# Layer A's attention: block scores inside each tile's near score products, block values inside the near value batch, outputs in the two halves of one PSUM bank

## The chip, the core and the metric

The kernel runs on one core of one Trainium2 chip. The metric is device time in microseconds (us) of one execution; less is better. The engines: PE multiplies matrices (PEld are its weight loads), DVE is the vector engine, ACT the scalar engine with the exponential, POOL the general one, SP issues most of the DMA transfers. Every engine works through its own row of instructions in a fixed order and waits on semaphores for the others. SBUF is the on-chip memory of 128 partitions; PSUM, in eight banks of 128 x 512 float32, takes what PE computes.

## What is computed

A decoder trunk of two layers over x of 1 x 1024 x 1024 (float32). Layer A has a sparse attention with three branches, layer B a dilated attention across shared keys; after each stands a SwiGLU. The change touches layer A's attention alone:

```
def nsa_attention(h, ...):                    # 16 heads of 64, in 4 groups that share keys
    ...
    k_cmp = compress(kvh(kc), pe_k, w1_k, w2_k)         # 63 blocks of 32 tokens, stride 16
    v_cmp = compress(kvh(vc), pe_v, w1_v, w2_v)
    s = einsum('bsgrd,bngd->bgrsn', q, k_cmp) * scale   # block scores
    p, denom, _ = masked_softmax(s + bias_c, dist_c >= 0)
    p_cmp = p / maximum(denom, 1e-30)
    o_cmp = einsum('bgrsn,bngd->bsgrd', p_cmp, v_cmp)   # block values
    imp = einsum('bgrsn,nj->bgsj', p_cmp, overlap)      # what a query makes of each 64-token block
    score = where(forced, imp + FORCE_BONUS, where(blk_j <= cur, imp, -1.0))
    _, sel_idx = top_k(score, 8)
    ...                                                 # o_sel: attention to the 8 chosen blocks ("far")
    o_win, _ = banded_attention(q, kwn, vwn, 255, 1, rel_bias)    # the last 256 tokens ("near")
    o = g[..., 0:1] * o_cmp + g[..., 1:2] * o_sel + g[..., 2:3] * o_win
    return o @ w_out
```

## The kernel before

Layer A's attention runs over 32 units: 4 groups g of heads by 8 tiles t of 128 queries. A unit has four heads, taken in two pairs hp. Queries and keys are kept as a high and a low part in the reduced format fp32r. The high and low part of a query stand above each other on 128 partitions (Q); a key part is loaded twice, into both halves of the partitions, so that two products (key part high, key part low) with the same Q give the full score.

`cmp_job` (L709) makes a unit's block scores: four products of plain float32, Q against the 63 block keys kc (L718, 128x64), two heads to a score bank; DVE adds the bias C and takes the row minimum (L726), ACT the exponential (L730), POOL scales by gate and denominator (L740, L741). From tile 4 on a chain of small DVE instructions ranks the blocks and writes the mask mk (L745 to L756), PE turns it (L758) and ACT copies it into the queries' extra rows QM (L759). `dense_job` (L769) makes two heads' scores of one branch: near (br = 2, at most three key blocks; L795 and L796 against the tiles KW) or far (br = 1; the tiles K with KF or QM); DVE adds the bias T or TW (L798), ACT takes the exponential (L804), POOL scales (L808). A job's second half, `back()`, comes later: `values` (L345) turns the weights P block by block on PE (`turned`, L327, into a pt bank), DVE and ACT by turns copy them to the tiles pT (L330), and PE multiplies by the value block, one product for each of the two head pairs, onto 64 partitions each (L361). The block values have a product of their own over all 128 partitions (L765), which opens the output bank. Outputs go through two banks "o"; DVE copies them to oT (L818).

Score banks are three, pt banks three. Near keys come by `load_kw`: once for tiles 0 to 3 of a group (512 columns), once for tiles 4 to 7 (768 columns). The order is that of `jobs()`: near pair 0, the next unit's block scores, near pair 1, far pairs 0 and 1, with back halves two jobs later; a scheduler then interleaves the engines' rows from this order and from its own costs. Layer B's attention further on uses the same `values` and `turned`, and writes its outputs to the two halves of one bank (copy at L1641).

Of the kernel before, what the change touches and what calls it, by code (L numbers as in the profile page):

```python
# [24 lines left out]
G = 4  # L25
# [90 lines left out]
def trunk(ctx, tc, I, out):  # L116
# [206 lines left out]
    def turned(p, heads, copy):  # L323

        ps = bank("pt")
        for i, h in enumerate(heads):
            prev = nc.tensor.transpose(ps[:, i * 128:(i + 1) * 128], h, ident)  # L327
        w = len(heads) * 128
        t = p.tile([128, 512], F32, name="pT", bufs=6)
        copy(t[:, :w], ps[:, :w])  # L330
        return t, prev
# [13 lines left out]
    def values(p, po, Ps, vs, first, last, behind=None):  # L345
# [5 lines left out]
        for lo, hi in zip([0] + ends, ends):  # L351
# [6 lines left out]
            for b in reversed(range(lo, hi)):  # L358
                with after(prev), after(behind if lo == 0 and b == hi - 1 else None):
                    for e in range(2):  # L360
                        mm = nc.tensor.matmul(po[64 * e:64 * e + 64, :256], vs[b], ts[b - lo][:, e * 256:(e + 1) * 256],  # L361
                                              start=first and lo == 0 and b == hi - 1, stop=last and hi == nb and b == lo,
                                              skip_group_check=True)
                prev = mm
# [29 lines left out]
    kc = ares.tile([128, G, DH], F32, name="kc")  # L394
# [5 lines left out]
    with ExitStack() as c:  # L400
# [98 lines left out]
        def compress(i, kc2, weights):  # L499
# [25 lines left out]
            if i == 0:  # L525
# [8 lines left out]
                nc.vector.tensor_copy(kc, ps2.rearrange("p (g n) -> p g n", n=DH))  # L534
# [96 lines left out]
    with ExitStack() as c:  # L631
# [8 lines left out]
        rKw = [Ring(f"KW{i}", [128, (512, 768)[i]], F32R, [((kA0, kA1)[i], 2)]) for i in range(2)]  # L640
# [3 lines left out]
        rW = Ring("TW", [128, 384], F32, [(kA1, 4), (kB, 1)])  # L644
# [57 lines left out]
        pcs = [wk.tile([128, 4, 64], F32, name=f"pc{i}") for i in range(2)]  # L702
        units = [(g, t) for g in range(G) for t in range(NT)]
        po_, weights = {}, [None, None]
# [6 lines left out]
        def cmp_job(g, t):  # L711
            C = grp["C", g]
            nv = min(8 * t + 7, 63)
            psv = []
            for hp in range(2):
                ps = bank("s")[:].rearrange("p (e n) -> p e n", e=2)
                for e in range(2):
                    nc.tensor.matmul(ps[:, e, :DH], f32(query(g, t, 2 * hp + e)), kc[:, g, :], start=True, stop=True)  # L718
                    psv.append(ps[:, e, :])
            pc = pcs[(g * NT + t) % 2]  # L720
            pv = pc[:, :, :nv]
            nc.gpsimd.memset(pc[:, :, nv:64], 0.0)
            mx = wk.tile([128, 4], F32, name="cm", bufs=3)
            dn = wk.tile([128, 4], F32, name="cd", bufs=3)
            for hh in range(4):
                nc.vector.tensor_tensor_reduce(out=pc[:, hh, :nv], in0=psv[hh][:, :nv],  # L726
                                               in1=C[:, hh, 56 - 8 * t:56 - 8 * t + nv], scale=1.0, scalar=3e38,
                                               op0=OP.add, op1=OP.min, accum_out=mx[:, hh:hh + 1])
# [13 lines left out]
            if t >= 4:  # L742
# [13 lines left out]
                nc.vector.tensor_scalar(mk, s2_, -2e38, BIG, op0=OP.is_gt, op1=OP.mult)  # L756
                mt = bank("pt")
                nc.tensor.transpose(mt[:16, :128], mk, ident)  # L758
# [3 lines left out]
            def back():  # L762
                pT, _ = turned(wk, [pc[:, 2 * c:2 * c + 2, :] for c in range(2)], nc.vector.tensor_copy)
                po = po_[g, t] = bank("o")
# [3 lines left out]
        def dense_job(g, t, br, hp):  # L768
# [42 lines left out]
            def back():  # L811
                if hp == 0:
                    return
# [1009 lines left out]
```

## Time and profile before

| | us |
|---|---|
| median of 3 runs (2864.04 to 2868.19) | 2866.13 |
| the profiled execution | 2866.31 |
| its span, first to last instruction | 2864.5 |
| layer A's attention in it, 280.34 to 697.67 | 417.33 |
| PE busy in this stretch | 408.87 |
| DVE, ACT, POOL busy in it | 327.54, 290.34, 221.64 |

In the profile's rows a group is named by line, engine and operation, out<-in by tile names, count, busy time and mean duration; behind the bar stands the idle time ahead of it and what ended that. In the order of time, a row is start, duration, engine, line, tiles, count, and in brackets a wait with its releaser. A wait row reads: who waited for whom, us in total, times, longest. A product of plain float32 has two records (so 128 block-score products are 256 records); a transpose has one.

### The profile page before, as it was taken

How to read it: one execution, taken by the hardware profiler on the slowest of the kernel's cores; microseconds unless marked ns; L12 is line 12 of the kernel's file. 1: busy time of each engine (PE TensorE's matmuls, PEld its weight loads, DVE VectorE, ACT ScalarE, POOL GpSimd, SP SyncE). 2: the span in 40 equal slices, each digit the busy share in tenths (PEclk: the TensorE clock that was granted, in tenths of full speed). 3: DMA queues.
4: the chain of work that ended last, by engine and by line, in shares of the span. 5: the costliest groups of instructions: out<-in, count | busy, mean ns of one | idle time of the engine just before them, and what ended most of it. 6: DMA issues, size and time to landing. Idle time of an engine off the chain costs nothing.

```text
span 2864.5 us, 43332 instructions
## 1 busy us (share of the span) xinstructions
PE 2782.1 (97%) x14686; PEld 2256.2 (79%) x14686; DVE 2248.1 (78%) x4563; ACT 1441.3 (50%) x3173; POOL 1463.9 (51%) x1502
## 2 busy tenths in 40 slices
PE   9999999999999999999999999999989999999997
PEld 8988777776778888888777788787767788888886
DVE  5443877877878989998885877588888788888987
ACT  5432767775563433343364444577756434343434
POOL 3135555553666555655557777210026656655552
PEclk9999999999999999999999999999999999999999
DMA  8669143112222232222223555776450221112112
GB/s 234 210 206 325 44 107 81 42 42 107 85 63 67 67 81 69 61 68 69 63 89 112 157 157 162 243 236 183 127 177 19 74 60 55 56 52 63 52 45 78
DMA packets 276030, 307.02 MB, mean 107 GB/s; under 512 B 39676, under 2 KB 210733, under 8 KB 275808
## 3 DMA queue, kind: packets, MB, share of 16 engines
q1 hardware_dynamic: 255344, 241.26, 28.5%
q0 software_dynamic: 20464, 62.99, 6.9%
q8 instruction: 116, 1.90, 0.3%
q14 instruction: 106, 0.87, 0.1%
HBM read 237.93 MB, written 81.95 MB: 112 GB/s over the span
## 4 chain that ended last, share of the span: by engine, by line
PE 79%; DVE 9%; DMA 3%; POOL 3%; issue 3%; ACT 2%; SPq 1%; POOLq 0%; DVEq 0%; ACTq 0%
PE ux L1071 16%; PE uy L1071 13%; PE dx L923 7%; PE o L361 6%; PE pt L327 6%; PE dr L923 5%; PE mm L203 3%; PE mm L204 3%; PE mm L205 3%; DVE pl L884 2%; PE s L795 2%; PE dr L1071 2%; PE s L796 2%; PE dx L1071 1%; PE s L1671 1%
## 5 line engine op out<-in xcount | busy, mean ns | idle before, releaser
L884 DVE TENSOR_TENSOR pl<-oT,ph 128x512 fp32r<-128x512 f32 x337 | 354.6, 1069 | 68.8 <-PE dr L923 17.4
L883 ACT ACTIVATE ph<-oT 128x512 fp32r<-128x512 f32 x347 | 211.8, 627 | 198.4 <-PE ux L1071 50.1
L808 POOL TENSOR_SCALAR P<-P,sm,gates 128x384 f32<-128x384 f32 (+7 forms) x256 | 182.1, 723 | 118.0 <-DVE sm L806 98.2
L884 DVE TENSOR_TENSOR pl<-oTb,ph 128x512 fp32r<-128x512 f32 x233 | 213.7, 939 | 28.3 <-PE dr L923 17.2
L883 ACT ACTIVATE ph<-oTb 128x512 fp32r<-128x512 f32 x239 | 145.5, 627 | 167.9 <-PE ux L1071 52.1
L327 PE MATMUL pt<-ident,P 128*128 128x128 f32 x1536 | 223.1, 278 | 2.2 <-DVE pT L330 1.5
L928 DVE TENSOR_TENSOR xr<-xr,dr 128x512 f32<-128x512 f32 x320 | 203.9, 678 | 17.6 <-PE dr L923 17.5
L327 PEld LDWEIGHTS pt<-ident,P 128*128 128x128 f32 x1536 | 172.8, 141 | 51.5 <-issue 36.6
L928 DVE TENSOR_TENSOR xr<-xr,dx 128x512 f32<-128x512 f32 x320 | 204.4, 677 | 1.6 <-PE dx L923 1.6
L804 ACT ACTIVATE P<-P,m 128x384 f32<-128x384 f32 (+7 forms) x256 | 170.7, 668 | 59.9 <-DVE m L802 25.1
L1255 POOL TENSOR_TENSOR oT<-oT,gffn 128x512 f32<-128x512 f32 x92 | 110.3, 1206 | 147.8 <-DMA oT<-in_ffn_w_up_dram 100.7
L330 DVE COPY pT<-pt 128x512 f32<-128x512 f32 (+1 forms) x224 | 143.8, 648 | 50.9 <-PE pt L327 49.1
L1255 POOL TENSOR_TENSOR oTb<-oTb,gffn 128x512 f32<-128x512 f32 x92 | 109.7, 1200 | 106.7 <-DMA oTb<-in_ffn_w_up_dram 59.7
L361 PE MATMUL o<-pT,V 128*64 128x256 f32 x1200 | 158.7, 390 | 1.3 <-ACT pT L330 1.1
L330 ACT COPY pT<-pt 128x512 f32<-128x512 f32 x192 | 110.7, 577 | 94.6 <-PE pt L327 93.7
L1633 ACT ACTIVATE P<-P,st 128x384 f32<-128x384 f32 (+2 forms) x256 | 139.5, 547 | 32.2 <-DVE st L1628 29.9
L1628 DVE CUSTOM_DVE_ANT_0 P<-s,T 128x384 f32<-128x384 f32 (+2 forms) x256 | 112.3, 478 | 10.6 <-DMA T<-s 3.6
L798 DVE CUSTOM_DVE_ANT_0 P<-s,T 128x128 f32<-128x128 f32 (+3 forms) x192 | 100.9, 549 | 16.9 <-PE s L796 10.5
L361 PEld LDWEIGHTS o<-pT,V 128*64 128x64 f32 x1200 | 74.5, 136 | 49.5 <-issue 7.1
L923 PE MATMUL dx<-ph 128*128 128x512 f32 x320 | 107.5, 390 | 0.4 <-ACT ph L883 0.4
L923 PE MATMUL dx<-ph,pl 128*128 128x512 f32 x320 | 107.0, 389 | 0.0
L883 ACT ACTIVATE ph<-wd 128x512 fp32r<-128x512 f32 x86 | 53.6, 628 | 99.1 <-PE ux L1071 48.5
(622 smaller groups left out, 8323.0 us busy)
## 6 DMA issues: line engine op xcount, KB each, us to landing
qB<-xr POOLq DMA_DIRECT2D x96, 256.0 KB, 5.0
oT<-in_ffn_w_up_dram SPq DMA_DIRECT2D x92, 256.0 KB, 2.9
oTb<-in_ffn_w_up_dram SPq DMA_DIRECT2D x92, 256.0 KB, 2.9
Q<-qB SPq DMA_DIRECT2D x40, 512.0 KB, 7.7
wd<-in_ffn_w_down_dram SPq DMA_DIRECT2D x66, 256.0 KB, 2.6
oT<-in_b_w_q_dram SPq DMA_DIRECT2D x48, 256.0 KB, 4.1
K<-kBs SPq DMA_DIRECT2D x40, 256.0 KB, 9.1
wraw<-in_a_w_in_dram SPq DMA_DIRECT2D x18, 512.0 KB, 7.4
```

The lines of the kernel that those rows point to most:

```text
L327: prev = nc.tensor.transpose(ps[:, i * 128:(i + 1) * 128], h, ident)
L330: copy(t[:, :w], ps[:, :w])
L361: mm = nc.tensor.matmul(po[64 * e:64 * e + 64, :256], vs[b], ts[b - lo][:, e * 256:(e + 1) * 256], start=first and lo == 0 and b == hi - 1 ...
L804: nc.scalar.activation(P[:, e, :n], P[:, e, :n], AF.Exp, bias=mm[:, e:e + 1], scale=-1.0, accum_out=sm[:, e:e + 1])
L808: nc.gpsimd.tensor_scalar(P[:, e, :n], P[:, e, :n], sm[:, e:e + 1], gt(g, t, br, 2 * hp + e, 1), op0=OP.mult, op1=OP.mult)
L883: nc.scalar.activation(h, src, AF.Copy)
L884: (eng or nc.vector).tensor_sub(l, src, f32(h))
L923: nc.tensor.matmul(banks[t], part(a, t)[u], b[v], start=z == 0 and onX != 2, stop=z == 2, skip_group_check=True)
L928: nc.vector.tensor_add(xs, xs, banks[t])
L1071: mm = nc.tensor.matmul(b, x[:, i * 128:(i + 1) * 128], ys[i], start=first and (z, i) == (0, 0), stop=(z, i) == (2, 3), skip_group_check=True)
L1255: nc.gpsimd.tensor_mul(v, v, gains[:, k:k + 4].unsqueeze(2).to_broadcast([128, 4, 128]))
L1633: nc.scalar.activation(P[:, e, :n], P[:, e, :n], AF.Exp, bias=stats[:, slot, hh:hh + 1], scale=-1.0, accum_out=stats[:, slot, 4 + hh:5 + hh])
```

## The change

The compressed block keys are kept as a high and a low part, kcs. `load_kw(i)` now loads near keys for one unit: 64 columns of block keys out of kcs, then the unit's own near keys (192 to 384 columns). `near_scores` makes one pair of products over both, and DVE reads the bank twice: near columns to P, block columns to pc. `block_weights` and `block_mask` are the remaining parts of cmp_job, `far_scores` and `far_values` those of dense_job for the far branch, their arithmetic as before. `near_values` hands the block values to `values` as a last item `more` of the near batch, as two products onto 64 partitions. Outputs take the halves of one bank by turns, score banks are four, pT buffers five in place of six (for layer B too), TW, P2 and pc have more buffers. The loop at the end writes out the order: in step i near scores of unit i + 2, mask and far scores of unit i, far values of unit i - 1, near values of unit i.

```diff
@@ turned, values
-        t = p.tile([128, 512], F32, name="pT", bufs=6)
+        t = p.tile([128, 512], F32, name="pT", bufs=5)
...
-            for b in reversed(range(lo, hi)):
-                with after(prev), after(behind if lo == 0 and b == hi - 1 else None):
-                    for e in range(2):
-                        mm = nc.tensor.matmul(po[64 * e:64 * e + 64, :256], vs[b], ts[b - lo][:, e * 256:(e + 1) * 256],
-                                              start=first and lo == 0 and b == hi - 1, stop=last and hi == nb and b == lo,
-                                              skip_group_check=True)
+            ops = [(vs[b], vs[b], ts[b - lo][:, :256], ts[b - lo][:, 256:]) for b in reversed(range(lo, hi))]
+            if more is not None and lo == 0:
+                ops.append(more)
+            for i, (*v, ta, tb) in enumerate(ops):
+                with after(prev), after(behind if lo == i == 0 else None):
+                    for e, t in enumerate((ta, tb)):
+                        mm = nc.tensor.matmul(po[64 * e:64 * e + 64, :256], v[e], t, start=first and lo == i == 0,
+                                              stop=last and hi == nb and i == len(ops) - 1, skip_group_check=True)
@@ compress
-                nc.vector.tensor_copy(kc, ps2.rearrange("p (g n) -> p g n", n=DH))
+                split(*kcs, ps2.rearrange("p (g n) -> p g n", n=DH))
@@ layer A's attention
-        rKw = [Ring(f"KW{i}", [128, (512, 768)[i]], F32R, [((kA0, kA1)[i], 2)]) for i in range(2)]
+        rKw = Ring("KW", half, F32R, [(kA0, 2), (kA1, 4)])
...
-        def load_kw(g, a):
-            cols = (slice(0, 512), slice(256, S))[a]
-            K = grp["KW", g, a] = [rKw[a].tile() for _ in range(2)]
+        def load_kw(i):
+            if i >= len(units):
+                return
+            g, t = units[i]
+            k0 = max(t - 2, 0) * 128
+            K = grp["KW", g, t] = [rKw.tile() for _ in range(2)]
+            n = max((t + 1) * 128 - k0, 192)
             for z in range(2):
-                load_k(K[z], kS[1, g, z][:, cols])
+                nc.sync.dma_start(f32(K[z][:, :DH]), f32(kcs[z][:, g, :]))
+                load_k(K[z][:, DH:DH + n], kS[1, g, z][:, k0:k0 + n])
...
+        o_ = psum["o"].tile([128, 512], F32, name="o", bufs=1)
+        outs, ends = Turns([o_[:, :256], o_[:, 256:]]), [None]
+        score_bank = lambda: psum["s"].tile([128, 512], F32, name="s", bufs=4)
...
-                for e in range(2):
-                    nc.tensor.matmul(ps[:, e, :DH], f32(query(g, t, 2 * hp + e)), kc[:, g, :], start=True, stop=True)
...
+        def near_scores(g, t, hp):
+            C, K = grp["C", g], grp["KW", g, t]
+            n = 128 * min(t + 1, 3)
+            w = max(DH + n, 256)
...
+                ps = score_bank()
+                for z in range(2):
+                    nc.tensor.matmul(ps[:, :w], q, K[z][:, :w], start=z == 0, stop=z == 1)
+                nc.vector.tensor_tensor_reduce(out=P[:, e, :n], in0=ps[:, DH:DH + n], in1=grp["TW", g, hh][:, 384 - n:],
+                                               scale=1.0, scalar=3e38, op0=OP.add, op1=OP.min, accum_out=mm[:, e:e + 1])
+                nc.vector.tensor_tensor_reduce(out=pc[:, hh, :nv], in0=ps[:, :nv],
+                                               in1=C[:, hh, 56 - 8 * t:56 - 8 * t + nv], scale=1.0, scalar=3e38,
+                                               op0=OP.add, op1=OP.min, accum_out=mx[:, hh:hh + 1])
...
-                po = po_[g, t] = bank("o")
-                nc.tensor.matmul(po[:, :256], vc[:, g, :], pT[:, :256], start=True, stop=False, skip_group_check=True)
...
+            ends[0] = values(wk, po, grp["P2", g, t], [grp["V", 1, g, b // 4][:, b % 4, :] for b in range(k0, t + 1)],
+                             True, False, ends[0], (vc[:, g, :64], vc[:, g, 64:], pT[:, :256], pT[:, :256]))
...
-        lag = [2]
-        pipelined(jobs(), lag)
+        for i in range(-2, len(units) + 1):
+            if 0 <= i < len(units):
+                loads(*units[i])
+            if i >= 0:
+                load_kw(i + 3)
+            for what, d in [('a', 2), ('m', 0), ('f', 0), ('v', -1), ('b', 2), ('c', 2), ('n', 0), ('g', 0)]:
+                if 0 <= i + d < len(units):
+                    steps[what](units[i + d])
```

The letters of the last loop: a and b are near_scores of head pairs 0 and 1, c block_weights, m block_mask, f and g far_scores, n near_values, v far_values.

**What moves on PE, the scores.** Before, PE's row at the near scores of group 0, tile 2 (KW near keys, Q queries, kc block keys, V far values):

```order
L795 MATMUL s<-KW_2720,Q_2683 128x384
L796 MATMUL s<-KW_2721,Q_2683 128x384
L795 MATMUL s<-KW_2720,Q_2685 128x384
L796 MATMUL s<-KW_2721,Q_2685 128x384
L361 MATMUL o<-pT,V_2737 64x256 x2
L718 MATMUL s<-kc,Q_2683 128x64
L718 MATMUL s<-kc,Q_2685 128x64
L718 MATMUL s<-kc,Q_2687 128x64
L718 MATMUL s<-kc,Q_2689 128x64
```

The same tile in the changed kernel, from its first row (K far keys):

```order
L746 MATMUL s<-KW_2749,Q_2687 128x448
L746 MATMUL s<-KW_2750,Q_2687 128x448
L746 MATMUL s<-KW_2749,Q_2689 128x448
L746 MATMUL s<-KW_2750,Q_2689 128x448
L833 MATMUL s<-K_2732,Q_2687 128x256
L833 MATMUL s<-K_2732,Q_2689 128x256
L746 MATMUL s<-KW_2749,Q_2691 128x448
L746 MATMUL s<-KW_2750,Q_2691 128x448
```

The four products with kc are gone, the near products are 64 columns wider, and they stand ahead of the far scores of tile 0.

**On PE, the values.** Before, the near values of group 1, tile 4 (VW near values, vc block values):

```order
L795 MATMUL s<-K_2905,Q_4218 128x512
L796 MATMUL s<-K_2906,QM_4222 128x512
L765 MATMUL o<-pT,vc 128x256
L361 MATMUL o<-pT,VW_4224 64x256 x2
L361 MATMUL o<-pT,VW_3788 64x256 x4
L795 MATMUL s<-K_2905,Q_4220 128x256
```

Now, the same tile, with the end of tile 3's far values ahead of it (first row), which fill the other half of the bank:

```order
L364 MATMUL o<-pT,V_2996 64x256 x4
L801 MATMUL pt<-ident,mk 16x128
L833 MATMUL s<-K_2990,Q_4301 128x256
L833 MATMUL s<-K_2990,Q_4301 128x512
L327 MATMUL pt<-ident,P_5024 128x128
L833 MATMUL s<-K_2990,Q_4303 128x256
L833 MATMUL s<-K_2990,Q_4303 128x512
L327 MATMUL pt<-ident,P_5024 128x128
L364 MATMUL o<-pT,VW_4311 64x256 x2
L364 MATMUL o<-pT,VW_3889 64x256 x4
L364 MATMUL o<-pT,vc 64x256 x2
```

The full-width product has become two half-width ones at the batch's end. Between the two batches stand the mask's transpose, far scores and turned weights of tile 5. Over the whole stage PE's row has 99 unbroken runs of half-width products before and 107 now.

**On SP.** The changed kernel's row where group 1 begins (kc0, kc1 block keys, kS near keys; KW4 and KW5 belong to group 1, tile 3, KW0 to tile 4, Q1 and T to the coming tiles of the group):

```order
L709 DMA VW00_3889<-vS_79 128x4x64
L704 DMA KW4_4327<-kc0_90 128x64
L320 DMA KW4_4327<-kS_78 64x384
L321 DMA KW4_4327<-kS_78 64x384
L704 DMA KW5_4328<-kc1_91 128x64
L320 DMA KW5_4328<-kS_78 64x384
L321 DMA KW5_4328<-kS_78 64x384
L659 DMA Q10_4301<-qS_77 128x512
L672 DMA T4_4636<-sA_73 128x512
L672 DMA T0_4313<-sA_73 128x512
```

Six transfers for a tile stand where the row before had four for half a group; at this place the near keys of tile 3 are ahead of the group's second half of queries.

More of the change, by code (lines that the diff above doesn't have):

```diff
@@ L343, in trunk, with values @@
     copies = [0]
-    def values(p, po, Ps, vs, first, last, behind=None):
+    def values(p, po, Ps, vs, first, last, behind=None, more=None):
         nb = len(vs)
@@ L393, in trunk @@
     gates = ares.tile([128, NT, 48], F32, name="gates")
-    kc = ares.tile([128, G, DH], F32, name="kc")
+    kcs = [ares.tile([128, G, DH], F32R, name=f"kc{z}") for z in range(2)]
     vc = ares.tile([128, G, 128], F32, name="vc")
@@ L721, in cmp_job, with block_tiles @@
+        def block_tiles(g, t):
+            nv = min(8 * t + 7, 63)
+            pc = pcs[(g * NT + t) % 3]
             pv = pc[:, :, :nv]
@@ L723, in cmp_job, with block_weights @@
             mx = wk.tile([128, 4], F32, name="cm", bufs=3)
+            blocks_[g, t] = pc, pv, mx, nv
+            return blocks_[g, t]
+        def block_weights(g, t):
+            pc, pv, mx, nv = blocks_[g, t]
             dn = wk.tile([128, 4], F32, name="cd", bufs=3)
[L725 to L728, printed above, removed]
             for hh in range(4):
@@ L864, in trunk, with far_values @@
-        lag = [2]
-        pipelined(jobs(), lag)
+            exponentials(P, n, mm, lambda e: gt(g, t, 1, 2 * hp + e, 1))
+            if hp == 1:
+                grp["P1", g, t] = weights[1, 0], weights[1, 1]
+        def far_values(g, t):
+            po = po_[g, t]
+            ends[0] = values(wk, po, grp["P1", g, t], [grp["V", 0, g, b // 4][:, b % 4, :] for b in range(t + 1)],
+                             False, True)
+            nc.vector.tensor_copy(oT[:, 2 * g:2 * g + 2, tok(t)], po.rearrange("p (c q) -> p c q", q=128))
@@ new lines, in loads @@
+        def loads(g, t):
+            if t == 0:
+                load_q(g, 1)
+                load_v(1, g, 1)
+                load_bias(g, 0)
+                load_v(0, g, 1)
+                if g == 0:
+                    for h in (4, 6):
+                        bias_skewed(sA, 0, LA, WA + 1, h, None)
+            elif g + 1 < G:
+                if g == 0 and 3 <= t < 7:
+                    bias_skewed(sA, 0, LA, WA + 1, 2 + 2 * t, None)
+                if t == 1:
+                    load_ks(g + 1)
+                    load_v(0, g + 1, 0)
+                elif t == 2:
+                    load_bias(g + 1, 1)
+                elif t == 4:
+                    load_q(g + 1, 0)
+                elif t == 6:
+                    load_kf(g + 1)
+                    load_v(1, g + 1, 0)
```

146 lines of the change are left out of this document (54 added, 92 removed).

## The prediction

> **What bounds the kernel now.** I read the page first, then the stretches of layer A's attention, then the order of time on PE.
>
> ```profile
> span 2864.5 us, 43332 instructions
> PE 2782.1 (97%) x14686; PEld 2256.2 (79%) x14686; DVE 2248.1 (78%) x4563; ACT 1441.3 (50%) x3173; POOL 1463.9 (51%) x1502
> 280.34:697.67 417.33, 408.87 (x2865) 302.11 (x2863) 327.54 (x1462) 290.34 (x903) 221.64 (x388) 1.00 0.22 59
> 678.00:698.00 20.00, 19.32 (x155) 12.84 (x154) 7.46 (x16) 9.05 (x16) 4.66 (x4) 1.00 0.16 54
> ```
>
> The third line is one stretch: its length, then busy time of PE, PEld, DVE, ACT and POOL, the granted clock, the DMA share. It runs from the first block score to the first product of the next stage, and holds all that the change rewrites. PE is busy 408.87 of 417.33 us at clock 1.00 (97.97%), DVE 78%, DMA 22%. So this stage lasts as long as PE's instructions one after another, and PE stands idle for 417.33 - 408.87 = 8.5 us in all. The last line, the final 20 us, holds hardly any score work (DVE 7.46): even there PE is full. What a PE instruction takes must be read start to start, since the durations shown overlap:
>
> ```profile
> 282.14 0.28 PE L796 MATMUL s<-KW,Q 128*128 128x256 f32 x1
> 282.26 0.28 PE L795 MATMUL s<-KW,Q 128*128 128x256 f32 x1
> 282.37 0.28 PE L796 MATMUL s<-KW,Q 128*128 128x256 f32 x1
> 282.49 1.00 PE L718 MATMUL s<-kc,Q 128*128 128x64 f32 x8
> 283.30 0.36 PE L795 MATMUL s<-KW,Q 128*128 128x256 f32 x1
> ...
> 296.66 1.10 PE L718 MATMUL s<-kc,Q 128*128 128x64 f32 x8
> 297.61 0.39 PE L327 MATMUL pt<-ident,pc 128*128 128x128 f32 x2
> ...
> 298.40 0.34 PE L795 MATMUL s<-KW,Q 128*128 128x384 f32 x1
> 298.57 0.34 PE L796 MATMUL s<-KW,Q 128*128 128x384 f32 x1
> 298.75 0.60 PE L327 MATMUL pt<-ident,P 128*128 128x128 f32 x4
> ...
> 677.65 0.60 PE L765 MATMUL o<-pT,vc 128*128 128x256 f32 x2
> 678.08 0.60 PE L327 MATMUL pt<-ident,P 128*128 128x128 f32 x4
> ...
> 681.08 1.08 PE L361 MATMUL o<-pT,V 128*64 128x256 f32 x8
> 682.10 1.09 PE L327 MATMUL pt<-ident,P 128*128 128x128 f32 x8
> 683.12 1.08 PE L361 MATMUL o<-pT,V 128*64 128x256 f32 x8
> 684.13 1.53 PE L327 MATMUL pt<-ident,P 128*128 128x128 f32 x12
> 685.59 1.51 PE L361 MATMUL o<-pT,V 128*64 128x256 f32 x12
> 687.04 1.53 PE L327 MATMUL pt<-ident,P 128*128 128x128 f32 x12
> ```
>
> A near product of 256 columns takes 0.115 us (282.14 to 282.26 to 282.37), one of 384 takes 0.175: 0.03 us for each 64 columns. The four block-score products of a tile (eight records) take 0.81 us (282.49 to 283.30) to 0.95 us (296.66 to 297.61).
>
> **The change, part by part.** *Block scores go.* 32 tiles lose eight records each. I take 0.87 us, between the two readings: **-27.8 us** (25.9 to 30.4).
>
> *Near products get wider.* 24 tiles with three key blocks go from 384 to 448 columns: 8 products x 0.03 x 24 = 5.8. Four tiles with t = 1 go from 256 to 320: 4 x 8 x 0.03 = 1.0. With t = 0 the width stays 256. **+6.8 us.** Weight loads of these products stay as many.
>
> *Block values join the near batch.* One full-width product took 0.43 us (677.65 to 678.08). Two half-width ones are four records; eight records of L361 take 1.02 us and twelve 1.45 (681.08 to 682.10, 685.59 to 687.04), so 0.108 each: 0.43. **0.**
>
> *The row of PE's work is cut otherwise.* From the same rows a run of half-width products costs a constant of 1.02 - 8 x 0.108 = 0.16 behind it, and the transposes ahead of it (eight in 1.02, twelve in 1.46, 0.11 each) another 0.14: 0.30 us per run, whatever its length. In PE's order of this stage there are 99 such runs before and 107 now, so **+2.4 us**. The sum so far is -27.8 + 6.8 + 2.4 = **-18.6 us**.
> The Trainium skill, TensorEngine Tiling (Array Packing), Key Properties, says that a change of tiling mode, not of the tile, drains TensorE. The trace agrees with 0.30 us; by that rule alone putting the block values beside the near ones would save 32 switches, but the count of runs rises, so the rule speaks against the change here; without it the sum would be -21.0.
>
> *Waits.* These are the rows in which PE's weight loads wait for a score bank, for the mask, or anything at all on PE:
>
> ```profile
> PEld s L795 <- DVE m L798: 9.6, 26, 0.7
> PEld s L795 <- DVE mp L798: 3.0, 9, 0.6
> PEld s L718 <- DVE m L798: 2.3, 7, 0.4
> PEld pt L758 <- DVE mk L756: 1.5, 4, 0.5
> PE pt L327 <- DVE pT L330: 1.5, 3, 0.8
> L818 DVE COPY oT<-o 128x256 f32<-128x256 f32 x32 | 13.4, 419 | 9.9 <-PE o L361 9.4
> ```
>
> Score banks: 9.6 + 3.0 + 2.3 = 14.9 us of weight loads waited for DVE to empty one. The change gives a fourth bank and takes two fewer per tile, since the block scores had two of their own; but a near bank is now read twice by DVE. The mask (1.5) is made two tiles ahead, so its chain on DVE is no longer what PE waits for. Against that: one pT buffer fewer (the 1.5 at L330 can grow), a far-key load that stands behind near loads at the start, and the output bank, which adds a wait. That last one: the first near product of a tile follows the copy of the tile before out of the same bank (L818, 419 ns). Behind it on PE stand the tile's transposes and scores, and DVE waits for those. Its cover is what PE does between the two batches, scores and transposes, in most tiles 1 us or more by the prices above. I cannot read the net: it is bounded by -14.9 (all bank waits go) and by +13.4 (all 32 copies lie open, x32 | 13.4). I take -4.4, about half of the 8.5 us in which PE stands idle, since more banks and more lead are nearest to the rows that wait most. DVE, ACT and POOL keep their instructions in this stage; their work stays hidden beside PE as long as DVE's 327.54 us fit under it: 83% of the new length. Layer B loses a pT buffer too, with as many runs (63) as before: 0, within 2 us either way.
>
> *Near keys for each tile.* SP issues six transfers per tile in place of the four per half group:
>
> ```profile
> KW<-kS SPq DMA_DIRECT2D x16, 192.0 KB, 3.6
> ...
> 412.50 0.45 SPq L320 DMA_DIRECT2D KW<-kS  x1
> 413.01 0.59 SPq L321 DMA_DIRECT2D KW<-kS  x1
> 413.69 0.55 SPq L320 DMA_DIRECT2D KW<-kS  x1
> 414.29 0.59 SPq L321 DMA_DIRECT2D KW<-kS  x1
> ...
> 402.03 0.43 DVE L818 COPY oT<-o 128x256 f32<-128x256 f32 x1 [0.48 <-PE o L361]
> 407.55 0.42 DVE L818 COPY oT<-o 128x256 f32<-128x256 f32 x1 [0.46 <-PE o L361]
> ...
> SPq L700 <- PE o L361: 173.6, 11, 41.2
> ```
>
> Four issues take 2.4 us, six 3.6, and the last lands about 3.6 us later: 7.2 us. Two short tiles (5.5 us each, from one copy to the next) are 11 us, and the buffers come free two tiles ahead of their use. Cost nothing; without that cover, see the third rival.
>
> The sum: -18.6 - 4.4 = -23.0 us, against the profiled execution's 2866.31 us (span 2864.5 and 1.8 around it), which is 0.2 above the median of the runs: **2843.3 us**. Smallest difference that a measurement of this kernel can tell: about 0.2%, 5.7 us.
>
> **The rivals.**
> *DVE takes part of it back.* PE loses 23 us, DVE nothing; at 83% with an order that is fixed on both engines, each bank comes later relative to PE. Price: the 8.5 us of waits double instead of halving, -18.6 + 8.5 = -10.1: 2856. For: DVE already ends 14.9 us of waits. Against: fewer banks taken per tile.
> *The shared output bank lies open.* -18.6 + 13.4 = -5.2: 2861. Against it, the cross-layer in this same profile already writes its outputs to the two halves of one bank, and PE is hardly held by the copies:
>
> ```profile
> L1641 DVE COPY o<-o x32: 627/640/695, 1841.5 to 2076.6; 128x256 f32<-128x256 f32 x32
> ...
> who waited for it (us, times):
>   PEld uy L203: 0.3, 1
> ```
>
> The Trainium skill, PSUM — Partial Sum Buffer, PSUM bank collisions raise a hardware error, says to guard by bank and quadrant, not by address. By it the wait is real, 2861 if nothing covers it; the rows of the cross-layer show the guard without its price.
> *Near keys come late (slower).* A value load on SP waits for the far values of the tile before: 11 such waits of 15.8 us in the mean (173.6 in 11, at most 41.2). If the next tile's near keys stand behind it, they come 15.8 + 7.2 - 11 = 12 us late at each of three changes of group: 2843 + 36 = 2879. It decides where near keys due within two tiles stand in SP's row behind such a wait of over 4 us (11 - 7.2). Against it: in SP's row two or three tiles' near keys stand ahead of those value loads.
> *Nothing comes of it.* What PE loses returns as waits on the chain from scores through exponentials to transposes: 2866. Against it PE's 98% and the last 20 us.
>
> **How the numbers follow.** Forecast 0.66, DVE rival 0.14, output bank 0.06, nothing 0.08, near keys 0.06. The likeliest gives 2843.3. The range takes in the bounds of the waits, -33.5 (2832.8) and -5.2 (2861.1), widened by 2 at the low end for layer B and by 1 at the high one: 2831 to 2862; it leaves out the last two rivals. Faster by over 0.2% (under 2860.6): forecast, DVE rival and half of the output bank, 0.83. Within: the rest of that and most of "nothing", 0.10. Slower: 0.07.
>
> **What would show it.** The group of eight 128x64 records per tile is gone, and 128x448 products stand 0.205 us apart; the stage is near 394 us long; PE's idle time in it is under 8.5 us, with fewer weight loads ended by L798's successor. Wrong would be: near products that wait for a DMA of KW (third rival), half-width products that wait for the copy to oT (second), a stage as long as before with more idle time on PE (fourth), or a change of over 2 us outside the stage.

## The result, and the profile after

| | before | changed |
|---|---|---|
| runs, median (lowest to highest), us | 4, 2867.08 (2864.04 to 2868.19) | 4, 2849.47 (2848.69 to 2851.01) |
| ratio to before, 95% interval | 1 | 0.9941 (0.9924 to 0.9958) |
| the profiled execution | 2866.31 | 2848.69 |
| layer A's attention in it | 417.33 | 401.54 |

The change makes the kernel 17.6 us faster by the medians (0.59%, and 0.42% at the least by the interval); 23.0 were forecast. First the page of the changed kernel, and its stretches: the whole stage (first near score to first product of the next stage), its first 30 us, and the rest. The columns are those of the stretches shown before.

```profile
span 2846.9 us, 43111 instructions
PE 2762.8 (97%) x14494; PEld 2234.4 (78%) x14494; DVE 2234.1 (78%) x4563; ACT 1439.8 (51%) x3174; POOL 1467.4 (52%) x1502
278.95:680.49 401.54, 386.52 (x2674) 277.50 (x2672) 322.38 (x1462) 288.05 (x903) 226.32 (x400) 0.98 0.31 88
278.95:308.95 30.00, 22.11 (x101) 16.62 (x101) 20.96 (x131) 24.30 (x101) 22.71 (x55) 0.79 0.75 203
308.95:680.49 371.54, 364.40 (x2575) 260.88 (x2571) 301.42 (x1332) 263.74 (x803) 203.61 (x345) 1.00 0.28 79
```

The same split of the kernel before:

```profile
280.34:310.34 30.00, 28.12 (x180) 22.50 (x179) 23.46 (x140) 25.16 (x105) 19.53 (x44) 0.94 0.32 89
310.34:697.67 387.33, 380.75 (x2687) 279.61 (x2685) 304.07 (x1323) 265.19 (x800) 202.11 (x345) 1.00 0.21 57
```

The stage is 15.8 us shorter; the other 1.8 us of the profiled executions lie outside it. PE is busy 22.35 us less (408.87 to 386.52), but stands idle 15.0 us in place of 8.5. Where that idle time lies is plain: in the first 30 us it is 7.9 us (30.00 - 22.11) in place of 1.9, at a granted clock of 0.79 in place of 0.94, with 101 instructions done in place of 180; in the rest it is 7.1 in place of 6.6.

Idle time misses a slow clock and what overlapped durations hide, so from here on I use two numbers that come from starts alone. **Price**: each PE instruction of the stage at its start-to-start time where nothing holds it: 0.112 us for a block-score record, 0.007 + 0.00043 per column for other score products, 0.109 for a transpose, 0.108 for a half-width value record, 0.216 for a full-width one, and 0.30 per run of half-width products. **Loss**: what the row of starts takes beyond that.

| us | before | changed | difference |
|---|---|---|---|
| block-score records, 256 to 0 | 28.7 | 0 | -28.7 |
| 640 other score products | 110.2 | 116.3 | +6.2 |
| value records, full width, 64 to 0 | 13.8 | 0 | -13.8 |
| value records, half width, 912 to 1040 | 98.5 | 112.3 | +13.8 |
| runs, 99 to 107 | 29.7 | 32.1 | +2.4 |
| **price** (with 992 transposes; ends as in the trace) | 388.7 | 368.6 | **-20.1** |
| **loss**, first 30 us of the stage | 5.9 | 15.4 | **+9.5** |
| **loss**, later | 22.4 | 17.3 | **-5.1** |

So PE's work shrank as forecast, and so did the later waits; the start of the stage gave 9.5 us back. These are PE's rows there, with the idle time ahead of a row in brackets:

```profile
278.95 0.87 PE L746 MATMUL s<-KW,Q 128*128 128x256 f32 x6
282.21 4.08 PE L746 MATMUL s<-KW,Q 128*128 128x256 f32 x14 [2.39 <-DVE stl L170]
...
289.33 0.69 PE L327 MATMUL pt<-ident,pc 128*128 128x128 f32 x2 [1.44 <-POOL pc L780]
...
292.20 0.80 PE L834 MATMUL s<-KF,Q 128*128 128x256 f32 x2 [1.33 <-DMA KF<-kS]
...
305.78 0.44 PE L327 MATMUL pt<-ident,P 128*128 128x128 f32 x2 [2.52 <-POOL P L730]
```

Four waits, 7.7 us. Three of them lead to loads that SP issued late, two by way of POOL; the second, for the block weights pc, isn't followed further here:

```profile
277.83 0.23 POOL L681 COPY C<-T 128x31 f32<-128x31 f32 x1 [7.62 <-DMA T<-sA]
278.31 1.04 POOL L383 DMA_DIRECT2D qS<-stl  x2 [0.25 <-issue]
...
281.46 0.69 DVE L170 SCALAR_TENSOR_TENSOR stl<-mm,sth 128x512 fp32r<-128x512 f32 x1 [6.43 <-DMA qS<-stl]
...
270.07 4.35 SPq L672 DMA_DIRECT2D T<-sA  x4
274.70 0.37 SPq L709 DMA_DIRECT2D V<-vS  x1
282.62 0.49 SPq L704 DMA_DIRECT2D KW<-kc  x1
...
289.05 0.44 SPq L320 DMA_DIRECT2D KF<-kS  x1
...
296.76 2.90 SPq L672 DMA_DIRECT2D T<-sA  x4
```

The near keys of units 1 and 2, twelve transfers, stand ahead of the far bias T (270.07; in the kernel before the same four went out at 259.60). POOL waits 7.62 us for that bias with the store of stl behind it, DVE's stl waits for the store, and the first near bank waits on DVE behind stl: PE's 2.39 us. Then SP waits from 275.1 to 282.62 for a KW buffer, and the far keys KF, whose buffer was free long before (in far_keys_first below they go out at 276.48), go out at 289.05. The weights that PE gets late at 305.78 stand in POOL's row behind TW of the next group (L676), whose T went out at 296.76.

Over the whole stage PE's weight loads waited so:

```profile
PEld o L364 <- ACT pT L330: 6.2, 16, 0.9
PEld pt L327 <- POOL P L730: 4.6, 5, 2.8
PEld pt L327 <- DVE pT L330: 3.5, 10, 0.6
PEld o L364 <- DVE pT L330: 2.9, 8, 0.6
PEld s L833 <- DVE cm L749: 2.7, 7, 0.8
...
PEld o L364 <- DVE oT L848: 0.5, 2, 0.3
...
PEld s L746 <- DMA KW<-kS: 0.4, 1, 0.4
```

The 14.9 us of waits for a score bank have become 2.7 (cm L749 is the last reader of a near bank). The copy out of the shared output bank cost 0.5 us in 32 tiles, and near keys came late once, by 0.4.

### The profile page after: what moved, and what is told of

It reads as the page before. It is cut to its first block, busy times and chain, and to the rows that moved or that the text cites. A ratio compares the mean times of both kernels' runs of the same rounds, so it can differ in the third digit from the quotient of the medians.

```text
span 2846.9 us, 43111 instructions
## 1 busy us (share of the span) xinstructions
PE 2762.8 (97%) x14494; PEld 2234.4 (78%) x14494; DVE 2234.1 (78%) x4563; ACT 1439.8 (51%) x3174; POOL 1467.4 (52%) x1502
## 3 DMA queue, kind: packets, MB, share of 16 engines
q1 hardware_dynamic: 272240, 249.40, 29.2%
## 4 chain that ended last, share of the span: by engine, by line
PE 84%; DVE 7%; ACT 2%; issue 2%; POOL 1%; DMA 1%; SPq 1%; DVEq 0%; ACTq 0%; POOLq 0%
PE ux L1098 18%; PE uy L1098 14%; PE dx L950 7%; PE o L364 7%; PE pt L327 6%; PE dr L950 5%; PE dr L1098 4%; PE mm L203 3%; PE mm L204 3%; PE mm L205 3%; DVE pl L911 2%; PE s L746 2%; PE dx L1098 1%; PE s L834 1%; PE s L1678 1%
## 5 line engine op out<-in xcount | busy, mean ns | idle before, releaser
L911 DVE TENSOR_TENSOR pl<-oTb,ph 128x512 fp32r<-128x512 f32 x233 | 213.0, 937 | 28.3 <-PE dr L950 17.3
L327 PE MATMUL pt<-ident,P 128*128 128x128 f32 x1536 | 229.5, 279 | 5.4 <-POOL P L730 2.5
L955 DVE TENSOR_TENSOR xr<-xr,dr 128x512 f32<-128x512 f32 x320 | 204.0, 679 | 17.8 <-PE dr L950 17.6
L1282 POOL TENSOR_TENSOR oTb<-oTb,gffn 128x512 f32<-128x512 f32 x92 | 110.2, 1206 | 106.3 <-DMA oTb<-in_ffn_w_up_dram 81.5
L1655 DVE CUSTOM_DVE_ANT_0 P<-s,T 128x384 f32<-128x384 f32 (+2 forms) x256 | 112.3, 478 | 9.8 <-PE pt L327 4.4
L835 DVE CUSTOM_DVE_ANT_0 P<-s,T 128x128 f32<-128x128 f32 (+3 forms) x192 | 99.7, 550 | 10.3 <-PE s L834 10.1
```

Source lines behind the costliest of these rows:

```text
L911: (eng or nc.vector).tensor_sub(l, src, f32(h))
L955: nc.vector.tensor_add(xs, xs, banks[t])
L1282: nc.gpsimd.tensor_mul(v, v, gains[:, k:k + 4].unsqueeze(2).to_broadcast([128, 4, 128]))
```

## The experiments

All times are ratios to the kernel before, run beside each of them on the same chip. The medians in us below come from several chips, so runs of different sections are compared by their ratios and by their stage. This table is the summary; each run is told below. Price, losses and stage come from one trace of each.

| kernel | price | loss, first 30 us | loss, later | stage | ratio (95%) |
|---|---|---|---|---|---|
| before | 388.7 | 5.9 | 22.4 | 417.3 | 1 |
| changed | 368.6 | 15.4 | 17.3 | 401.5 | 0.9941 (0.9924 to 0.9958) |
| changed_again | 368.6 | 12.6 | 16.8 | 398.3 | 0.9934 (0.9918 to 0.9951) |
| far_keys_first | 368.6 | 12.7 | 18.6 | 400.1 | 0.9942 (0.9928 to 0.9955) |
| far_keys_and_bias_first | 368.6 | 10.3 | 17.0 | 396.2 | 0.9934 (0.9920 to 0.9948) |
| three_score_banks | 368.9 | 13.5 | 32.8 | 415.5 | 0.9996 (0.9987 to 1.0006) |
| three_score_two_output_banks | 369.2 | 13.3 | 33.4 | 416.2 | 0.9987 (0.9976 to 0.9997) |
| before_four_score_banks | 389.0 | 5.4 | 15.3 | 410.0 | 0.9965 (0.9952 to 0.9978) |
| block_scores_apart | 389.9 | 9.0 | 22.9 | 422.1 | 1.0030 (1.0021 to 1.0039) |
| six_pT_buffers | 368.6 | 12.6 | 17.1 | 398.6 | 0.9939 (0.9927 to 0.9951) |
| block_values_apart | 368.3 | 12.2 | 12.1 | 392.9 | 0.9911 (0.9899 to 0.9924) |
| block_values_first | 375.5 | 12.4 | 9.5 | 397.7 | 0.9937 (0.9921 to 0.9953) |
| loads_first_and_values_apart | 368.3 | 9.1 | 12.0 | 389.7 | 0.9898 (0.9883 to 0.9912) |

One caution holds for all: any edit makes the scheduler lay PE's row anew, so a difference of a microsecond or two in loss needn't be the edit's own.

### Is it the start? far_keys_first, far_keys_and_bias_first

```
             if i >= 0:
-                load_kw(i + 3)
+                with after(grp["KF", 0, "end"] if i < 4 else None):
+                    load_kw(i + 3)
```

where "end" is the last transfer of KF; and for the second one also (the loop then begins its loads at unit 1)

```
         load_kf(0)
-        for i in (1, 2):
-            load_kw(i)
         load_v(1, 0, 0)
         load_v(0, 0, 0)
+        loads(*units[0])
+        for i in (1, 2):
+            load_kw(i)
```

> The near keys of units 3 to 6 are issued by SP behind the loads of the far keys KF of group 0, in place of ahead of them; nothing else changes. Start theory: the first 30 us of the stage lose about 10 us more than before the change, and part of it is SP's row: KF is issued at 289.05 because SP waits from 275.1 to 282.6 for a KW buffer and then issues two units of near keys. With KF ahead, PE's wait of 1.33 us for KF and the one of 2.52 us at 305.8 (POOL behind a bias load that SP also issued late, at 296.76) go, and some of the slow clock: 4 to 6 us less than the changed kernel's 2849.5, so 2843.5 to 2845.5. Rival, the waits were mis-sized over the whole stage (the start only moves): within 1.5 us of 2849.5.

> As far_keys_first, and the loads of unit 0's far bias T (four transfers), of the second queries and of the values are issued ahead of the near keys of units 1 and 2. Start theory: POOL no longer waits 7.62 us for that bias, the store behind it and DVE's stl come on time, and PE's first wait (2.39 us) goes too: 6 to 9 us less than 2849.5, so 2840.5 to 2843.5. Rival (the start only moves its waits): within 1.5 us of 2849.5; a second rival, near keys of unit 1 now come late for near scores that are next in PE's row: a new wait of 1 to 5 us for KW, and no gain over far_keys_first.

The first gained nothing: 0.9942, median 2850.17. KF went out at 276.48, and the waits for KF and for P are gone as expected (0.4 us is left of the 2.52), but the first wait, which it left alone, was longer in this execution (rows of SP, POOL and PE):

```profile
276.48 0.45 SPq L320 DMA_DIRECT2D KF<-kS  x1
...
278.25 0.23 POOL L681 COPY C<-T 128x31 f32<-128x31 f32 x1 [6.50 <-DMA T<-sA]
...
285.55 4.42 PE L746 MATMUL s<-KW,Q 128*128 128x256 f32 x14 [4.19 <-DVE stl L170]
```

With the bias first too, the first 30 us lose 10.3 in place of 15.4 or, in the changed kernel's second trace (changed_again below), 12.6:

```profile
261.42 3.23 SPq L672 DMA_DIRECT2D T<-sA  x4
...
275.68 0.51 SPq L320 DMA_DIRECT2D KF<-kS  x1
...
268.21 0.23 POOL L681 COPY C<-T 128x31 f32<-128x31 f32 x1 [0.91 <-DMA T<-sA]
...
283.07 2.79 PE L746 MATMUL s<-KW,Q 128*128 128x256 f32 x14 [0.71 <-DVE stl L170]
...
289.45 0.44 PE L327 MATMUL pt<-ident,pc 128*128 128x128 f32 x2 [1.45 <-POOL pc L780]
```

The wait for stl is 0.71 us there, but that can't be put down to the edit. These are PE's waits at the start of the second trace of the unaltered changed kernel:

```profile
PE s L834 <- DMA KF<-kS: 2.8, 1, 2.8
PE pt L327 <- POOL P L730: 2.3, 1, 2.3
...
PE s L746 <- DVE stl L170: 0.7, 1, 0.7
```

SP issued the bias T there at 270.59, as late as in the first trace, and POOL waited 3.78 us for it, yet PE's wait for stl was 0.70; it was 0.70 too in six_pT_buffers, block_values_apart and block_values_first, with the same order of loads. So the chain over the bias, POOL and the store held PE in two traces (2.39 and 4.19 us) and not in the others, while the waits for KF and for P came back in the second trace and are gone with the edit.

The rivals' "within 1.5 us" isn't met in the stage (5.3 and 2.1 us below the two traces of the changed kernel), nor is the 6 to 9 us of the start theory in the time: median 2847.32, an interval that overlaps the changed kernel's. What stays is PE's wait for the first block weights from POOL (1.45), a new wait of 1.31 us for a pT copy, and the clock. The last run below prices the load order better.

### What is the fourth score bank worth? three_score_banks, three_score_two_output_banks, before_four_score_banks

```
-        score_bank = lambda: psum["s"].tile([128, 512], F32, name="s", bufs=4)
+        score_bank = lambda: psum["s"].tile([128, 512], F32, name="s", bufs=3)
```

and for the second one the outputs by turns in two banks:

```
-        outs, ends = Turns([o_[:, :256], o_[:, 256:]]), [None]
+        o2_ = psum["o"].tile([128, 512], F32, name="o2", bufs=1)
+        outs, ends = Turns([o_[:, :256], o2_[:, :256]]), [None]
```

> The changed kernel with three score banks in place of four; outputs stay in the two halves of one bank, one PSUM bank is unused. Theory that the fourth bank took PE's waits for DVE (9.6 + 3.0 + 2.3 us of weight loads before, 2.7 + 1.2 after): most come back, 3 to 8 us more than 2849.5, so 2852.5 to 2857.5. Rival, that two banks fewer taken per tile and the written order did it: within 1.5 us of 2849.5.

> As three_score_banks, and outputs by turns in two banks of their own. This gives the price of the shared output bank against three_score_banks. Forecast of the prediction (the copy is covered by scores and transposes between the batches): within 1.5 us of three_score_banks. Rival (shared bank lies open): 5 to 13 us less than three_score_banks.

Both theories were far too small. Without the fourth bank the whole change is worth nothing (0.9996): PE's price is as low as in the changed kernel, and its later loss is 32.8 us in place of 17.3. Only a small part of it appears at the banks (after the first 30 us PE waited 2.6 us for the last reader of a near bank, 0.2 in the changed kernel). The row of weight loads that grew most is transposes, for weights that reached POOL late; the scores behind these were late too, since DVE waited 16.2 us for far scores (L834) in place of 8.9:

```profile
PEld pt L327 <- POOL P L730: 11.4, 15, 2.7
```

In the changed kernel that row read 4.6 us in 5 waits, the longest at the start. The two rows are weight loads' waits, and they don't add up to the 15.5 us. So "nothing comes of it", a rival of the prediction with a chance of 0.08, is what the change does without its fourth bank. Separate output banks on top gave 0.9987 and the same stage (416.2): the shared output bank costs nothing that these runs can show, with three score banks at least.

The converse is the kernel before with the changed kernel's banks alone (score_bank and outs as there, for the block scores too):

```
-                    ps = bank("s")
+                    ps = score_bank()
...
-                po = po_[g, t] = bank("o")
+                po = po_[g, t] = outs()
```

> The kernel before with nothing of the change but its banks: four score banks in place of three, and outputs by turns in the two halves of one bank. After three_score_banks (2866.05: the change without its fourth bank gives nothing) two theories stand. Bank alone: the fourth bank is worth some 15 us in either order, since PE's waits for DVE cost 22 us in the stage before; then 2849 to 2857, and the merged products are worth only the rest. Pair: the merged products make the fourth bank necessary, since DVE now empties a near bank in two reads, and before the change two short block banks per tile cost little; then 2861 to 2867.

(This kernel leaves out what orders the output batches of neighbouring units in the shared bank: in PE's row a tile's block-value product stands ahead of the near values of the tile before. So its outputs aren't the layer's attention, and what such an order would cost isn't in its time; PE's, DVE's and ACT's instructions in the stage are those of the kernel before.) It is faster, by 10.0 us (0.9965): between the two theories, nearer to the bank alone. The later loss fell from 22.4 to 15.3 us, the stage by 7.3:

```profile
278.49:688.51 410.02, 401.42 (x2865) 304.15 (x2863) 325.21 (x1462) 289.27 (x903) 221.70 (x388) 1.00 0.22 60
```

The four corners together, in loss after the first 30 us: the kernel before, 22.4 with three banks and 15.3 with four; the changed kernel, 32.8 and 17.3. The bank is worth 7 us in the old kernel and 15.5 in the new one. With three banks the rest of the change loses 10.4 us more than the kernel before, half of the 19.8 that PE saves (388.7 - 368.9), and 7.6 more in the first 30 us. Which part of it loses the 10.4, the merged score products, the joined batch or the written order, these runs don't separate.

### Do PE's prices add up? block_scores_apart

```
-            w = max(DH + n, 256)
+            w = max(n, 256)
...
+            pb = score_bank()[:].rearrange("p (e n) -> p e n", e=2)
+            for e in range(2):
+                nc.tensor.matmul(pb[:, e, :DH], f32(query(g, t, 2 * hp + e)), f32(kcs[0])[:, g, :], start=True, stop=True)
...
```

> The changed kernel with the block scores as products of their own again (float32, two heads to a score bank, the high part of the block keys alone, so the block branch is computed with less precision), near products narrow again, near keys with the same loads and 256 columns at t = 0; four score banks, the rest as changed. By the prices of the prediction -27.8 + 6.8 is given back: +21, so 2868 to 2873 if PE's work adds up in full. Rival, the bank is all that counts and PE has slack: under 2860.

The stage took 422.1 us, 20.5 and 23.8 more than the two traces of the changed kernel; the price, which is only counted, rose by 21.3 (389.9 - 368.6), and the losses together (31.9) stayed near the 32.7 and 29.4 of those two traces, so PE's work adds up in full. In time it is slower than before by 0.30%, some 25 us above the changed kernel by the two ratios where 21 were expected, and its median of 2876.65 lies above the 2868 to 2873; outside the stage executions differ by more than that (below). The block scores are the whole gain on PE, and the other parts alone don't pay.

### Two small terms: six_pT_buffers, block_values_apart

```
-        t = p.tile([128, 512], F32, name="pT", bufs=5)
+        t = p.tile([128, 512], F32, name="pT", bufs=6)
```

> The changed kernel with six buffers pT in place of five. In the changed kernel PE and its weight loads waited for pT copies 6.2 + 3.5 + 2.9 us in the stage, against 3.0 + 2.6 + 1.9 before. If the missing buffer makes these: 2 to 5 us less than 2849.5. Forecast of the prediction (a pT buffer costs nothing): within 1.5 us of 2849.5.

0.9939, later loss 17.1: the missing buffer costs nothing here. Layer B's attention doesn't feel it either. Its stretch, from the first score to the first product behind, is 267.63 us before, 265.94 with five buffers, and 267.07 with six, one fence for each kernel:

```profile
1824.88:2092.51 267.63, 260.48 (x2089) 209.47 (x2088) 216.80 (x751) 202.11 (x614) 23.99 (x33) 0.99 0.68 201
```

```profile
1807.09:2073.03 265.94, 260.04 (x2090) 208.93 (x2088) 215.03 (x751) 201.66 (x614) 24.04 (x33) 0.99 0.67 202
```

```profile
1809.71:2076.78 267.07, 260.78 (x2089) 208.53 (x2087) 216.11 (x751) 201.95 (x614) 24.08 (x33) 0.99 0.68 202
```

The block values apart again:

```
+            with after(ends[0]):
+                pv_ = nc.tensor.matmul(po, vc[:, g, :], pT[:, :256], start=True, stop=False, skip_group_check=True)
             ends[0] = values(wk, po, grp["P2", g, t], ...,
-                             True, False, ends[0], (vc[:, g, :64], vc[:, g, 64:], pT[:, :256], pT[:, :256]))
+                             False, False, pv_)
```

> The changed kernel with the block values as one product over all 128 partitions again, ahead of each near batch in the same half bank. By the prices (0.43 us either way, as many runs of half-width products): within 2 us of 2849.5. Rival, the changes of tile shape cost by themselves: if the join saved 32 of them at 0.15 us each, +5.

The surprise of the study: 0.9911, median 2843.12, below the changed kernel's ratio, with an interval that just touches its interval; beside six_pT_buffers on the same chip (0.9939, the changed kernel but for one buffer) the intervals don't overlap. The stage is 8.7 and 5.4 us shorter than the two traces of the changed kernel. The price is the same (368.3), as the prediction had it; the later loss is 12.1 in place of 17.3 and 16.8.

```profile
279.33:672.21 392.88, 381.93 (x2609) 276.12 (x2607) 325.63 (x1462) 288.13 (x903) 222.73 (x394) 0.99 0.33 89
309.33:672.21 362.88, 357.65 (x2488) 258.48 (x2486) 303.46 (x1323) 262.33 (x795) 200.89 (x342) 1.00 0.29 81
```

PE's idle time after the first 30 us is 5.2 us (362.88 - 357.65) against 7.1. Where the loss went can be read from the starts. Beyond the prices, and after the first 30 us, the changed kernel's row has 28 gaps of over 0.2 us, 11.2 us in all; this one has 14, with 6.1.

A smaller part stands at the starts of near batches: seven of them came over 0.2 us late in the changed kernel, 2.7 us in all, and four here, 1.3, two of these at the block-value product itself. A joined batch opens with the pT that was copied last, and waits for that copy; a block-value product ahead of it needs a pT copied long before.

More stands at transposes and at the scores shortly behind them: 5.9 us in 15 gaps, and 2.6 in five here. The clearest case is the mask's transpose at tile 7 of each group, first in the changed kernel, then here:

```profile
366.69 0.27 PE L801 MATMUL pt<-ident,mk 128*16 128x128 f32 x1
367.49 0.30 PE L327 MATMUL pt<-ident,P 128*128 128x128 f32 x1 [0.53 <-ACT pT L330]
...
364.23 0.27 PE L801 MATMUL pt<-ident,mk 128*16 128x128 f32 x1
364.34 0.69 PE L811 MATMUL o<-pT,vc 128*128 128x256 f32 x2
364.87 0.27 PE L327 MATMUL pt<-ident,P 128*128 128x128 f32 x1
```

The next transpose waits for a pt bank that a pT copy has yet to empty (0.26 to 0.70 us in the four groups, 2.1 in all, and the same with six buffers pT). Here the scheduler has put the block-value product into that gap in all four groups, and nothing waits.

### Is it that cover, and do the gains add? changed_again, block_values_first, loads_first_and_values_apart

The first is the changed kernel unaltered. The second puts the pair of block-value products at the head of the joined batch:

```
-                ops.append(more)
+                ops.insert(0, more)
```

The third has the edits of far_keys_and_bias_first and block_values_apart together.

> The changed kernel once more, unaltered, beside the next two on one chip, so that these are compared with it there: 2846 to 2852. Its trace says how far the stage's 401.5 us and the 15.4 us that its first 30 us lose repeat: start theory 11 to 16 us of loss in the first 30 us again, and a stage of 398 to 403 us.

> The changed kernel with the block values as the first pair of products of the joined near batch in place of the last. block_values_apart (2843.1, stage 392.9) had 8.4 us fewer waits at the same work. Cover theory: a block-value product ahead of the batch, whose pT was copied long before, covers the copy of the near weights' last pT, and it does so as half-width products too: 2843 to 2847, near-batch starts lose under 1 us beyond 30 us of the stage (2.7 us in 7 cases in the changed kernel). Rival, it is the full-width shape or another order that the schedule takes: 2848 to 2852.

> far_keys_and_bias_first and block_values_apart together. If the start's loads and the cover of the copies are two causes: the first 30 us lose 8 to 11 us and the rest 11 to 13, stage 387 to 392 us, 2838 to 2842 (6 or more below the changed kernel). If both came from one place, no better than block_values_apart: 2842 to 2845.

changed_again: median 2847.86 (2842.84 to 2857.05), 0.9934. Its first 30 us lost 12.6 us, its later loss was 16.8 against 17.3, so that part repeats within half a microsecond, the start within three.

```profile
281.11:679.42 398.31, 383.70 (x2674) 275.03 (x2672) 322.14 (x1462) 287.88 (x903) 222.37 (x393) 0.99 0.32 88
```

block_values_first came out at 0.9937 (2849.47), no gain, as the rival said. Yet the later loss fell by 7.3 us, to 9.5, so there is a cover in half-width products too. It isn't where the theory had it: no near batch begins late after the first 30 us, but three of them wait behind the pair, about 2 us in all (the longest 0.58, for a pT copy), against 2.7 at the starts in the changed kernel. What the pair covers, like the full-width product, are the transposes: at tile 7 of each group it stands behind the mask's transpose, and no gap is left there. But the schedule now puts other work between the pair and the rest of its batch, so PE's row has 130 runs of half-width products in place of 107. In that row (names as in the code, KF the far keys):

```
L364 MATMUL o<-pT,vc 64x256 x2
L834 MATMUL s<-KF_2738,Q_2687 128x256
L834 MATMUL s<-KF_2738,Q_2689 128x256
L364 MATMUL o<-pT,VW_2757 64x256 x2
```

23 runs at 0.30 us are 6.9, and that is what came back: in this kernel's row, too, a run costs 0.09 us ahead of it and 0.20 behind it, in the median. A full-width product takes the same 0.43 us and needs no run of its own; between two transposes its start and its end cost nothing beyond that. In this the rival's full-width shape was right.

loads_first_and_values_apart beat everything: median 2838.32 (2837.19 to 2839.40), 0.9898, against 0.9934 of the changed kernel on the same chip, with intervals that don't overlap; 9.5 us below it and 29.2 below the kernel before, and all as expected: time, stage and both losses.

```profile
279.49:669.16 389.67, 380.88 (x2609) 274.77 (x2607) 323.23 (x1462) 288.18 (x903) 221.12 (x387) 1.00 0.32 88
279.49:309.49 30.00, 25.69 (x142) 17.96 (x141) 25.40 (x143) 26.85 (x110) 22.96 (x49) 0.94 0.66 178
```

Beside block_values_apart it differs by the load order alone: first 30 us 9.1 in place of 12.2, later 12.0 in place of 12.1, the stage 3.2 us shorter. So the two causes are separate, and the order of the loads is worth some 3 us of the 7 to 9.5 by which the start got worse (one trace each; the two ratios' intervals overlap). The first 30 us still lose 3 us more than before the change (9.1 against 5.9), and no run shows how to get these back.

## Why the prediction was right, and where not

The sign, the place (layer A's attention, PE's row) and the range held; the time came out 6.2 us above the forecast in the first runs. That is closer than the steps were. Price and waits were forecast at -18.6 and -4.4; in the first trace they were -20.1 and +4.4 (9.5 - 5.1), and another 1.8 us came from outside the stage, where none was forecast. These 1.8 are luck: the time outside the stage reaches from 2447.2 us to 2458.7 in two traces of the same changed kernel. By its steps:

- **Block scores go, -27.8.** Right: -28.7 by 256 records at 0.112, and block_scores_apart brought it back.
- **Near products wider, +6.8.** Right: +6.2. Four 448-wide products take 0.9 us in a row, what they enter from included, as here at 415.49 and 398.35.

```profile
398.35 1.06 PE L746 MATMUL s<-KW,Q 128*128 128x448 f32 x4
399.25 0.28 PE L833 MATMUL s<-K,Q 128*128 128x256 f32 x1
...
415.49 1.05 PE L746 MATMUL s<-KW,Q 128*128 128x448 f32 x4
416.37 0.39 PE L833 MATMUL s<-K,Q 128*128 128x512 f32 x1
```

- **Block values join the batch, 0.** Right as PE's work (13.8 us either way) and wrong as a whole: block_values_apart saves 5 us of later loss at the same price. A product of its own can stand where PE would wait for a copy, at the transposes above all; joined, it stands at the end of its batch. In the kernel before neither near batches nor the transposes behind the mask's have a gap of over 0.2 us after the first 30 us. The prediction asked what the new records take, not what the old product hid. Of the 5 us some 3 are traced to transposes and the scores behind them and 1.4 to batch starts; how much of these is that cover, and how much the new layout of the row, isn't separated.
- **More runs, +2.4.** Right: 107 were counted and 107 are there, and block_values_first shows the same price from another side. Only its halves were taken wrong: 0.16 behind a run and 0.14 ahead of it were read, 0.20 and 0.09 are the medians of the starts.
- **Waits, -4.4.** Here is the miss. In the stage behind its first 30 us the term was right (-5.1, and -5.6 in the second trace). The first 30 us weren't priced at all: "a far-key load that stands behind near loads at the start" was named and left in a lump with the rest, and they cost +9.5 (+6.7). SP's order was in hand, and the wait for a KW buffer ahead of KF, which held PE in both traces, could be read from it. The other chain, from twelve early transfers over the bias, POOL's row and the store to DVE, cost 2.39 us in the first trace and 0.70 in the second.
- **The reason given for those waits** was also half right. The fourth bank and the two banks fewer per tile were counted as two gains; three_score_banks shows a loss of 10.4 us from the rest of the change, and a gain of 15.5 from the bank, and only their sum is near -4.4.
- **Near keys per tile, 0, and layer B, 0.** Right: one wait of 0.4 us for KW in the rows, and layer B within 2 us.

The rivals. PE's idle time nearly doubled, 8.5 to 15.0 us, which is the price that "DVE takes part of it back" had; but it doubled in the first 30 us and at SP and POOL, and behind that it rose by 0.6 us, so that rival's mechanism isn't what happened. Of the forecast's own signs the fewer bank waits came; a stage near 394 us and less than 8.5 us of idle time on PE did not (401.5 and 398.3 us, 15.0 and 14.6). The shared output bank (0.5 us of waits, and no difference between one bank and two) and late near keys fell. "Nothing comes of it" is true of the change with three score banks.

## What to carry over

Work taken off a full engine is collected only if the buffers ahead of it let the next work start earlier: ask of each merge what now holds a buffer longer, and test the merge and the extra buffer one without the other. When a product is removed or joined, ask what copy it covered, not only what its records take. Read the first tens of microseconds of a stage as a stage of their own, with every queue's row from the first load on: there no lead has been built up, and a load that costs nothing later can stop an engine. And take a second trace before you name a chain: of the waits at this start one shrank from 2.39 us to 0.70 in the same kernel.

## What the runs showed of the hardware that wasn't expected

A short wait of PE costs more than its length. Behind the wait of 2.39 us the granted clock was 0.55 for 3.8 us, and 0.61 behind the next ones, though no gap between two starts up to there was longer than 2.7 us. The 14 products that took 4.08 us behind that wait took 2.79 in the second trace, behind a wait of 0.70, at a clock of 1.00:

```profile
282.21:286.00 3.79, 3.79 (x14) 3.66 (x15) 3.43 (x34) 3.61 (x21) 3.75 (x12) 0.55 0.80 219
286.00:292.20 6.20, 3.34 (x14) 2.04 (x12) 4.08 (x21) 4.09 (x20) 5.00 (x12) 0.77 0.58 179
292.20:297.30 5.10, 5.09 (x22) 3.62 (x22) 3.44 (x24) 3.64 (x16) 1.76 (x4) 0.61 1.03 237
```

The 320-wide products in the first of these rows stand 0.27 us apart where 0.145 is their price. Of the 15.4 us that the start lost, 7.7 are the four waits; the slow clock in these three rows is up to 3.79 x 0.45 + 6.20 x 0.23 + 5.10 x 0.39 = 5.1 more, and the end of these 30 us, 306 to 308.95 at 0.56, up to 1.3. The Trainium skill, TensorE: Matmul & The Clock Gate, What's actually happening, says that the clock is halved after an idle window of about 3.4 us that runs freely. The trace agrees on the half (0.50 from 290 to 294); here a gap of 2.7 us was enough.

And the same code takes different times from one execution to the next: from the end of this stage to layer B's first score 1126.6 us in the changed kernel's first trace and 1134.2 in its second, and between 1128 and 1135 in the other traces of the changed code. The six runs of changed_again reach from 2842.84 to 2857.05. That is why the stage's own numbers carry the argument here, and a few microseconds of one whole run none.
